# Later fetches of branch operands and gates, reordered remainder products and a shorter way for the softmax sums in a one-layer mixer trunk

## The chip, the core and the metric

The kernel runs on one core of a Trainium2 chip. The metric is the device time of one execution in microseconds, the median of several runs. The engines of the core are named as in the profile: PE (TensorE, with PEld for its weight loads), DVE (VectorE), ACT (ScalarE), POOL (GpSimd) and SP (SyncE, which here issues nearly all DMA transfers).

## The reference, cut to what matters

One layer on 1024 tokens of width 1024, with 16 learned tokens put in front (1040 positions). One projection makes the inputs of four mixers, their gate paths and four merge gates; the mixers' outputs are projected back, gated, summed and projected once more.

```python
h = rms_norm(h_res, pre_norm_g[i])
z = h @ w_in[i]
(pv, pg, cq, ckv, kr, mg, cu, cg, sbcx, sg, gl) = split_cols(z)

y_a = (pool_mixer(pv, pool_w[i], pool_scale[i]) * silu(pg)) @ w_out_pool[i]
y_b = (mla_attention(cq, ckv, kr, ...) * silu(mg)) @ w_out_mla[i]
y_c = (conformer_conv(cu, ...) * silu(cg)) @ w_out_conf[i]
y_d = (short_conv(sbcx, sc_dw_w[i]) * silu(sg)) @ w_out_sc[i]

gts = sigmoid(gl + gate_bias[i]).reshape(b_, l_, N_BRANCH, D_MODEL)
m = gts[:, :, 0] * y_a + gts[:, :, 1] * y_b + gts[:, :, 2] * y_c + gts[:, :, 3] * y_d
h_res = h_res + rms_norm(m @ w_o[i], post_norm_g[i])
```

Inside `mla_attention`, eight heads attend causally over keys and values that come out of a normalised low-rank `ckv`:

```python
kv = (rms_norm(c_kv, kv_norm_g) @ w_ukv).reshape(b_, l_, MLA_HEADS, QK_NOPE + V_DIM)
s = jnp.einsum('bqhd,bkhd->bhqk', qb, k)
s = jnp.where(k_pos[None, :] <= q_pos[:, None], s, -jnp.inf)
p = jax.nn.softmax(s, axis=-1)
o = jnp.einsum('bhqk,bkhd->bqhd', p, v)
```

## The kernel before

Every product is made of float32 values split into a high part and a remainder, and a product of two such values is three matmuls: high by high, high by remainder, remainder by high. The kernel has three stages, each with its own pools. The first makes the input projection by products of 512 columns into the PSUM banks `ps_pa` to `ps_pd`, and in between them, in four `lane`s of small steps, the norms, convolutions and the keys, values and queries, which it writes to DRAM. The second is the attention over 8 heads by 2 halves of the queries (16 units, `seq`). In between its products stand those of three of the four branches (`fills`, 48 steps spread over 112 blocks): for each branch 8 output tiles `d` of two halves, six matmuls of 512 columns each into `ps_y`, with the weights `whl`, the branch's operand `bo` (two tiles of 1 MB) and the gate `th`. The third stage makes the attention's output projection (`ps_u`) and the last projection.

No instruction is placed by hand. Each call records an operation in a `Plan`, and `flush` then orders them all by a list scheduler of its own: each engine takes, of the operations that its own costs say are ready, the one that was recorded first (moved by `ahead`). `late(ns)` tells it that a result is there so much later, `slow(ns)` that a DMA's is, and `behind` ties a transfer to the PE operation recorded last before it. The chip then executes each engine's instructions strictly in that order. Of the transfers, no more than eight may be under way in the scheduler's account, and eight semaphores in turn hold them to that on the chip.

What the change touches:

- `rs_row`, lines 943 to 969: the inverse root of a row of mean squares. PE multiplies with `ones` into a narrow bank, DVE scales (`rs`), POOL raises to the power -0.5, and PE transposes the result back into a row. `task_kv` (line 1274) calls it three times for `ckv`.
- `attend(h, c)`, lines 1506 to 1544: one unit. For each block `j` of 128 keys, three score matmuls into `ps_s`, the exponential on ACT, a split into the tile `pt` (four buffers), and three matmuls into `ps_o`: two with the whole 128 columns of `v_` as weights, and one, the remainder's product, with 64. Row 64 of the output holds the softmax sum. Blocks on the causal diagonal have fewer query columns: the last five blocks of a unit have 512, 400, 272, 144 and 16. The last, of 16 keys, is one matmul with `pz` and `vs`. `copy(ol[h][:, c], po)` then evacuates the bank.
- `sums(h)`, lines 1546 to 1556: for heads 0 to 6, row 64 of `ol` goes to DRAM (`l_dram`), from there to `lc` on 32 partitions, DVE takes the reciprocal, `lc` goes to DRAM (`r_dram`) and comes back broadcast over 64 partitions as `rb`. `head_out` multiplies `ol` with `rb` into `op` on DVE, and for odd heads with the gate `smg` on POOL. The last head makes its sums on PE (`sums_pe`) instead.
- `fills`, line 1605: the operand of the next branch is fetched at the tile `d == 4` of the current one.
- the loop over the units, line 1669: the gate `smg` of an odd head is fetched at its first unit.

Of the kernel before, what the change touches and what calls it, by code (L numbers as in the profile page):

```python
# [25 lines left out]
ALU = mybir.AluOpType  # L26
# [4 lines left out]
P = 128  # L31
# [440 lines left out]
def trunk_kernel(ctx, tc, a):  # L472
# [467 lines left out]

    done = {"ckv", "kr"}

    def rs_row(sqs, of, scale=None, tag="x"):

        n = sqs[0].shape[1]
        p = min(n, P)
        if len(sqs) > 1:  # L950
            add(POOL, sqs[0], sqs[0], sqs[1])
        sq = sqs[0]
        pc = bank(tag)[:p, :n // p]
        for j in range(n // p):
            PE.matmul(pc[:, j:j + 1].in_order(), sq[:, p * j:p * (j + 1)], ones, start=True, stop=True,
                      skip_group_check=True)
        yield
        rs = col([P, 4], "rs")[:p, :n // p]
        DVE.tensor_scalar(rs, pc, 1.0 / of, EPS, op0=ALU.mult, op1=ALU.add)
        POOL.tensor_tensor(rs, rs, mhalf[:p, :n // p], op=ALU.pow)  # L960
        if scale:
            DVE.tensor_scalar(rs, rs, scale, None, op0=ALU.mult)
        yield
        out = bank(tag)[:, :n]
        for j in range(n // p):
            PE.transpose(out[:, p * j:p * (j + 1)], rs[:, j:j + 1].to_broadcast([p, P]), ident[:p, :p])
        yield
        return out
# [275 lines left out]
    def task_kv():  # L1244
# [27 lines left out]
        ACT.activation(sq, ckv, AF.Square)  # L1272
        yield
        for n0, n in CH_KV:
            rs = yield from rs_row([sq[:, n0:n0 + n]], P)
            DVE.scalar_tensor_tensor(ckv[:, n0:n0 + n], ckv[:, n0:n0 + n], par[:, R_KVG:R_KVG + 1], rs,
                                     op0=ALU.mult, op1=ALU.mult)
        yield
# [227 lines left out]
    def attend(h, c):  # L1506

        q_, k_, v_ = qt[h, c], kt[h % 2], vt[h % 2]
        po = bank("o")
        nj = 4 * c + 5  # L1510
        for j in range(nj):
            lo_ = max(512 * c, P * j - NM)
            n = 512 * (c + 1) - lo_
            kn = P if j < nj - 1 else NM
            ks = slice(P * j, P * j + kn)
            qs = slice(512 - n, 512)
            s = bank("s")[:kn, :n]
            PE.matmul(s, k_[:NA, 0, ks], q_[:NA, 0, qs], start=True, stop=False)
            PE.matmul(s, k_[:QK, 0, ks], q_[:QK, 1, qs], start=False, stop=False)
            PE.matmul(s, k_[:QK, 1, ks], q_[:QK, 0, qs], start=False, stop=True)  # L1520
            d0 = P * j - NM
            dl, dh = max(d0, 512 * c, 0), min(d0 + P, 512 * (c + 1))
            if dh > dl:
                sd = s[:, dl - lo_:dh - lo_]
                add(DVE, sd, sd, maskT[:kn, dl - d0:dh - d0])
            p32 = at.tile([P, 512], F32, tag="p32", bufs=3, name="p32")[:kn, :n]
            ACT.activation(p32, s, AF.Exp)
            o = po[:, lo_ - 512 * c:]
            if kn == NM:
                x = pz[(2 * h + c) % 3]  # L1530
                copy(x[:NM], p32)
                copy(x[64:], p32)
                sub(POOL, x[32:32 + NM], p32, f(x[:NM]))
                PE.matmul(o, vs[h % 2][:, c], x, start=False, stop=True, skip_group_check=True)
            else:
                pt_ = at.tile([P, 2, 512], F32R, tag="pt", bufs=4, name="pt")[:, :, :n]
                split(pt_[:, 0], pt_[:, 1], p32)
                PE.matmul(o, v_[:, j, :P], pt_[:, 0], start=(j == 0), stop=False, skip_group_check=True)
                PE.matmul(o, v_[:, j, :P], pt_[:, 1], start=False, stop=False, skip_group_check=True)
                PE.matmul(o[:64], v_[:, j, P:], pt_[:, 0], start=False, stop=False, skip_group_check=True)  # L1540
            yield
        if c == 0:
            ol[h] = at.tile([P, 2, 512], F32, tag="ol", bufs=2, name="ol")
        copy(ol[h][:, c], po)

    def sums(h):

        lc = at.tile([32, 32], F32, tag="lc", bufs=2, name="lc")
        rb = at.tile([64, 2, 512], F32, tag="rb", name="rb")
        with plan.slow(5000):  # L1550
            ld(l_dram[h].rearrange("(o n) -> o n", o=1), ol[h][64:65].rearrange("p j n -> p (j n)"))
            ld(lc, l_dram[h].rearrange("(p n) -> p n", n=32))
            DVE.reciprocal(lc, lc)
            ld(r_dram[h].rearrange("(p n) -> p n", n=32), lc)
            ld(rb.rearrange("p j n -> p (j n)"), r_dram[h].partition_broadcast(64))
        return rb[:, 0], rb[:, 1]
# [35 lines left out]
    def fills():  # L1592
# [9 lines left out]
        for bi, (gi, wname, b0) in enumerate(branches):  # L1602
            bo = [bos[bi, k] for k in range(2)]
            for d in range(KD):
                if d == 4 and bi < 2:
                    with plan.behind():
                        load_bo(bi + 1)
                th = fp.tile([P, NT], F32, tag="th", bufs=3, name="th")
# [51 lines left out]
    for i, (h, c) in enumerate(seq):  # L1660
        with plan.behind() if i else nullcontext():
            if i + 2 < len(seq):
                load_q(*seq[i + 2])
            if c == 0 and h + 1 < H:
                load_kv(h + 1)
                if i == 0:
                    with plan.behind():
                        load_v(1)
            if c == 0 and h % 2:
                smg[h] = at.tile([P, NT], F32, tag="smg", name="smg")  # L1670
                ld(smg[h], z_dram[f"mg{h // 2}"])
        for j, _ in enumerate(attend(h, c)):
# [260 lines left out]
```

## Time and profile before

| what | value |
|---|---|
| runs | 971.98, 972.14, 972.54 us; median 972.14 us |
| the profiled execution's own time | 970.57 us |
| its span, first to last instruction | 968.7 us |
| granted TensorE clock, mean | 0.997 |
| matmuls on PE | 5003 |
| DMA traffic | 203.06 MB, mean 210 GB/s |

In the profile a matmul's duration is modelled and overlaps that of the next one, so what a matmul costs is read from the distance of the starts: 12 matmuls of 512 columns in a row stand 2.72 us apart in the chain of waits. Nearly every operation is issued at one line of the kernel, line 362 in `issue`, so the rows are told apart by their tiles and not by their lines.

### The profile page before, as it was taken

Reading aid. Unit: us, or ns where it says so; the run is one execution under the profiler, and the core shown is the slowest. Engines: PE = TensorE matmul, PEld = TensorE weight load, DVE = VectorE, ACT = ScalarE, POOL = GpSimd, SP = SyncE. Lnnn points to the kernel's source line nnn. Section 1 sums busy time; section 2 is a strip of 40 time slices with the busy share of each in tenths; the row PEclk is TensorE's granted clock in tenths of the full one; section 3 lists DMA queues with packets and bytes.
Section 4 is the critical chain, followed back from the end, with each engine's and each line's share of the span. In section 5 each row is a group of like instructions: output and inputs, shape, how many; then the busy total and the mean of one; then the engine's idle time right before and its main releaser. Section 6 shows DMA issues by size and latency. Waiting matters only on the chain.

```text
span 968.7 us, 15229 instructions
## 1 busy us (share of the span) xinstructions
PE 953.4 (98%) x5003; PEld 810.9 (84%) x5003; DVE 703.8 (73%) x1113; ACT 450.8 (47%) x914; POOL 678.5 (70%) x628
## 2 busy tenths in 40 slices
PE   8999999999999999999999999999999999999996
PEld 8999899889888888888888888888888888788885
DVE  5956957978979985446554867346868887799867
ACT  7743244343344555444444444366375465225631
POOL 5957565666767797788779587565377686647965
PEclk9999999999999999999999999999999999999998
DMA  8145566677688677685656687799969863772644
GB/s 258 46 126 146 164 217 214 211 227 250 211 264 262 204 230 229 202 275 181 196 166 190 224 293 240 212 317 316 233 186 277 210 191 109 272 252 84 200 148 152
DMA packets 136343, 203.06 MB, mean 210 GB/s; under 512 B 19678, under 2 KB 83165, under 8 KB 135496
## 3 DMA queue, kind: packets, MB, share of 16 engines
q1 hardware_dynamic: 127288, 185.31, 62.5%
q10 hardware_dynamic: 8656, 15.74, 4.5%
q0 software_dynamic: 320, 1.05, 0.3%
q8 instruction: 39, 0.64, 0.3%
q14 instruction: 40, 0.33, 0.1%
HBM read 129.14 MB, written 72.90 MB: 209 GB/s over the span
## 4 chain that ended last, share of the span: by engine, by line
PE 85%; DVE 4%; DMA 4%; POOL 3%; issue 2%; ACT 1%; SPq 0%; DVEq 0%; POOLq 0%; ACTq 0%
PE ps_pa L362 15%; PE ps_pb L362 14%; PE ps_pc L362 14%; PE ps_o L362 9%; PE ps_u L362 8%; PE ps_y L362 7%; PE ps_s L362 7%; PE ps_pd L362 7%; PE ps_x L362 4%; DVE ps_w L362 1%; DMA qt<-q 1%; POOL S L362 1%; POOL A L362 1%; DMA whl<-w_out_pool 1%; DMA x<-in_x_dram 1%
## 5 line engine op out<-in xcount | busy, mean ns | idle before, releaser
L362 PE MATMUL ps_pb<-T,S 128*128 128x512 f32 (+2 forms) x792 | 173.6, 359 | 0.0
L362 PE MATMUL ps_pa<-B,A 128*128 128x512 f32 (+2 forms) x792 | 169.4, 359 | 0.0
L362 PEld LDWEIGHTS ps_pa<-B,A 128*128 128x128 f32 x792 | 134.3, 188 | 22.4 <-issue 1.0
L362 PEld LDWEIGHTS ps_pb<-T,S 128*128 128x128 f32 x792 | 134.5, 189 | 21.5 <-issue 0.5
L362 POOL TENSOR_TENSOR S<-ss,S 128x512 fp32r<-128x512 f32 x84 | 114.5, 1373 | 47.8 <-ACT S L362 46.9
L362 POOL TENSOR_TENSOR A<-raw,A 128x512 fp32r<-128x512 f32 x84 | 113.7, 1360 | 44.2 <-ACT A L362 43.0
L362 POOL TENSOR_TENSOR pt<-p,pt 128x512 fp32r<-128x512 f32 (+1 forms) x96 | 101.0, 1077 | 52.8 <-ACT pt L362 22.1
L362 DVE TENSOR_TENSOR u<-ps_pb,u 128x512 f32<-128x512 f32 (+2 forms) x66 | 40.3, 610 | 69.9 <-PE ps_pb L362 63.7
L362 DVE SCALAR_TENSOR_TENSOR ps_w<-conv,par,ps_w 128x512 f32<-128x512 f32 x116 | 87.2, 752 | 2.6
L362 PE MATMUL ps_y<-bo,whl 128*128 128x512 f32 x288 | 85.5, 405 | 0.8 <-DMA whl<-w_out_pool 0.8
L362 ACT ACTIVATE S<-ss 128x512 fp32r<-128x512 f32 x84 | 51.0, 629 | 74.4 <-DVE ss L362 49.7
L362 PE MATMUL ps_pc<-T,S 128*128 128x512 f32 (+1 forms) x396 | 85.2, 359 | 0.0
L362 PE MATMUL ps_pd<-T,A 128*128 128x512 f32 (+2 forms) x396 | 84.2, 358 | 0.0
L362 PE MATMUL ps_pc<-B,S 128*128 128x512 f32 (+1 forms) x396 | 84.0, 358 | 0.0
L362 ACT ACTIVATE p<-ps_s 128x512 f32<-128x512 f32 (+4 forms) x112 | 49.6, 444 | 59.9 <-PE ps_s L362 32.7
L362 PEld LDWEIGHTS ps_pd<-T,A 128*128 128x128 f32 x396 | 67.3, 189 | 10.8
L362 PEld LDWEIGHTS ps_pc<-T,S 128*128 128x128 f32 x396 | 66.7, 189 | 10.8
L362 PEld LDWEIGHTS ps_pc<-B,S 128*128 128x128 f32 x396 | 66.5, 189 | 10.4
L362 PE MATMUL ps_s<-qt,kt 100*128 100x512 f32 (+4 forms) x336 | 68.5, 325 | 1.0 <-DVE mxs L362 0.9
L362 PE MATMUL ps_o<-pt,vt 128*128 128x512 f32 (+7 forms) x288 | 67.6, 345 | 0.0
L362 PEld LDWEIGHTS ps_s<-qt,kt 100*128 100x128 f32 (+1 forms) x336 | 54.1, 176 | 12.0 <-DVE mxs L362 1.7
L362 ACT ACTIVATE A<-raw 128x512 fp32r<-128x512 f32 x84 | 51.9, 626 | 20.8 <-PE ps_pd L362 9.6
(281 smaller groups left out, 1905.0 us busy)
## 6 DMA issues: line engine op xcount, KB each, us to landing
raw<-in_w_in_dram SPq DMA_DIRECT2D x52, 512.0 KB
th<-th SPq DMA_DIRECT2D x32, 512.0 KB
th<-z ACTq DMA_DIRECT2D x60, 256.0 KB
v<-vhl SPq DMA_DIRECT2D x16, 384.0 KB
qt<-q SPq DMA_DIRECT2D x16, 384.0 KB
vt<-v SPq DMA_DIRECT2D x8, 768.0 KB
bo<-bo SPq DMA_DIRECT2D x6, 1024.0 KB
w_out_mla<-whl SPq DMA_DIRECT2D x16, 256.0 KB
```

The costliest lines, as they stand in the source:

```text
L362: getattr(self.handle[o["eng"]], o["op"])(*map(real, o["args"]), **{k: real(v) for k, v in o["kw"].items()})
```

## The change

Five edits. (1) `rs_row` takes a number `ns`, and `task_kv` passes 1500: the scheduler then takes both steps of the inverse root to be there 1500 ns later. (2) In `attend` the remainders' products of the last three 128-key blocks are kept in the list `thirds` and issued later: between the two products of the 144-column block, behind its second one, and behind the 16-column one. (3) The copy of the last head's output counts as 500 ns later. (4) `sums` goes from the SBUF row straight to the 32 partitions of `lc`; `l_dram` is no longer used. (5) The operand of the next branch is fetched at `d == 6`, and the gate of heads 1, 3 and 5 at the second unit of the head instead of the first.

```diff
-    def rs_row(sqs, of, scale=None, tag="x"):
+    def rs_row(sqs, of, scale=None, tag="x", ns=0):
...
-        DVE.tensor_scalar(rs, pc, 1.0 / of, EPS, op0=ALU.mult, op1=ALU.add)
-        POOL.tensor_tensor(rs, rs, mhalf[:p, :n // p], op=ALU.pow)
+        with plan.late(ns):
+            DVE.tensor_scalar(rs, pc, 1.0 / of, EPS, op0=ALU.mult, op1=ALU.add)
+            POOL.tensor_tensor(rs, rs, mhalf[:p, :n // p], op=ALU.pow)
...
-            rs = yield from rs_row([sq[:, n0:n0 + n]], P)
+            rs = yield from rs_row([sq[:, n0:n0 + n]], P, ns=1500)
...
         nj = 4 * c + 5
+        thirds = []
+
+        def rest(last=False):
+            PE.matmul(*thirds.pop(0), start=False, stop=last, skip_group_check=True)
+
...
-                PE.matmul(o, vs[h % 2][:, c], x, start=False, stop=True, skip_group_check=True)
+                PE.matmul(o, vs[h % 2][:, c], x, start=False, stop=False, skip_group_check=True)
+                rest(last=True)
...
                 PE.matmul(o, v_[:, j, :P], pt_[:, 0], start=(j == 0), stop=False, skip_group_check=True)
+                if j == nj - 2:
+                    rest()
                 PE.matmul(o, v_[:, j, :P], pt_[:, 1], start=False, stop=False, skip_group_check=True)
-                PE.matmul(o[:64], v_[:, j, P:], pt_[:, 0], start=False, stop=False, skip_group_check=True)
+                thirds.append((o[:64], v_[:, j, P:], pt_[:, 0]))
+                if j < nj - 4 or j == nj - 2:
+                    rest()
...
-        copy(ol[h][:, c], po)
+        with plan.late(500 if h == H - 1 else 0):
+            copy(ol[h][:, c], po)
...
-            ld(l_dram[h].rearrange("(o n) -> o n", o=1), ol[h][64:65].rearrange("p j n -> p (j n)"))
-            ld(lc, l_dram[h].rearrange("(p n) -> p n", n=32))
+            ld(lc, ol[h][64:65].rearrange("p j (a n) -> p (j a) n", n=32))
...
-                if d == 4 and bi < 2:
+                if d == 6 and bi < 2:
...
-            if c == 0 and h % 2:
+            if h % 2 and c == int(h < H - 1):
```

Since the scheduler orders everything anew, the order of the instructions differs on every engine from the first `rs` of `ckv` on. Three places show what matters.

The first is PE at the end of unit (head 0, second half). `ps_o` is the output bank, `pt` the split exponentials, `vt` the values, `pz` and `vs` the operands of the 16-column block; the first number after the names is the output's partitions, 64 for a remainder's product. Before:

```order
L362 MATMUL ps_o<-pt,vt_6875 128x272
L362 MATMUL ps_o<-pt,vt_6875 64x272
L362 MATMUL ps_o<-pt,vt_6875 128x144 x2
L362 MATMUL ps_o<-pt,vt_6875 64x144
L362 MATMUL ps_o<-pz_6929,vs_6861 128x16
L362 MATMUL ps_s<-qt,kt_6867 128x400 x3
```

and with the change:

```order
L362 MATMUL ps_o<-pt,vt_6875 128x272
L362 MATMUL ps_o<-pt,vt_6875 128x144
L362 MATMUL ps_o<-pt,vt_6875 64x400
L362 MATMUL ps_o<-pt,vt_6875 128x144
L362 MATMUL ps_o<-pt,vt_6875 64x272
L362 MATMUL ps_o<-pz_6929,vs_6859 128x16
L362 MATMUL ps_o<-pt,vt_6875 64x144
L362 MATMUL ps_s<-qt,kt_6867 128x400 x2
```

The two remainders' products of 400 and 272 columns now stand behind the two of 144, and the one of 144 behind that of 16.

The second is PE at the inverse roots of `ckv` in the first stage: `ones` by `sqk` makes the sums, `ident` by `rs` turns the roots back. Before:

```order
L362 MATMUL ps_x<-ones,sqk 128x1 x4
L362 MATMUL ps_pc<-B_325,S_1348 128x512 x9
L362 MATMUL ps_pa<-B_234,A_1412 128x256 x3
L362 MATMUL ps_x<-ident,rs 128x128 x4
L362 MATMUL ps_x<-ones,sqk 128x1 x4
L362 MATMUL ps_pa<-B_234,A_1412 128x256 x9
L362 MATMUL ps_pb<-T_564,S_1449 128x256 x8
L362 MATMUL ps_x<-ident,rs 128x128 x4
```

and with the change:

```order
L362 MATMUL ps_x<-ones,sqk 128x1 x4
L362 MATMUL ps_pc<-B_325,S_1348 128x512 x9
L362 MATMUL ps_pa<-B_234,A_1412 128x256 x12
L362 MATMUL ps_pb<-T_564,S_1449 128x256 x12
L362 MATMUL ps_pc<-T_531,S_1456 128x256
L362 MATMUL ps_x<-ident,rs 128x128 x4
L362 MATMUL ps_x<-ones,sqk 128x1 x4
L362 MATMUL ps_pc<-T_531,S_1456 128x256 x11
L362 MATMUL ps_pb<-T_316,S_1476 128x256 x12
L362 MATMUL ps_pd<-T_587,A_1505 128x256 x12
L362 MATMUL ps_pa<-B_257,A_1481 128x256 x8
L362 MATMUL ps_x<-ident,rs 128x128 x4
```

Nine 512-column and 25 256-column matmuls now stand between the first sums and their roots, where nine and three stood, and 43 between the second ones, where 17 stood.

The third is SP's queue early in the attention, where `whl<-w_out_pool` are the weights of the first branch, `bo` the operand of the second, `qt`, `kt`, `vt` and `vs` the tiles of the coming units, `smg` the gate of head 1. Before:

```order
L362 DMA smg<-z_mg_3488 128x1024
L362 DMA vt_6875<-v_2571 128x1536
L362 DMA vs_6861<-v_2571 16x2x128 x2
L362 DMA vs_6861<-v_2571 16x2x64
L362 DMA whl<-w_out_pool_987 128x512
L362 DMA th<-th_3863 128x1024
L362 DMA whl<-w_out_pool_1167 128x512
L362 DMA qt<-q_5195 96x1024
L362 DMA th<-th_4070 128x1024
L362 DMA whl<-w_out_pool_1408 128x512
L362 DMA l_7272<-ol 1x1024
L362 DMA bo<-bo_4590 128x2048
```

and with the change, first from the same `vt` on:

```order
L362 DMA vt_6875<-v_2611 128x1536
L362 DMA lc<-ol 32x1x32
L362 DMA whl<-w_out_pool_987 128x512
L362 DMA th<-th_3822 128x1024
L362 DMA whl<-w_out_pool_1167 128x512
L362 DMA th<-th_4100 128x1024
L362 DMA qt<-q_5020 96x1024
L362 DMA smg<-z_mg_3486 128x1024
L362 DMA whl<-w_out_pool_1408 128x512
```

and then, eight rows on, the place to which the operand of the second branch went:

```order
L362 DMA rb<-r_7339 64x1024
L362 DMA vs_6863<-v_2611 16x2x128 x2
L362 DMA vs_6863<-v_2611 16x2x64
L362 DMA vt_6904<-v_2611 128x1536
L362 DMA bo<-bo_4605 128x2048
L362 DMA bo<-bo_4808 128x2048
L362 DMA whl<-w_out_pool_1780 128x512
L362 DMA th<-th_4295 128x1024
L362 DMA lc<-ol 32x1x32
L362 DMA qt<-q_5020 96x1024
```

The gate moved from ahead of `vt` and the weights to behind them, and the pair `bo` from ahead of the tiles of head 3 to behind them.

## The prediction, made before the changed kernel was run

> **What bounds the kernel now.** I read the page first: the span, the busy time of each engine, and the chain.
>
> ```profile
> span 968.7 us, 15229 instructions
> PE 953.4 (98%) x5003; PEld 810.9 (84%) x5003; DVE 703.8 (73%) x1113; ACT 450.8 (47%) x914; POOL 678.5 (70%) x628
> ```
>
> PE is busy for all but 15.3 us, and nothing is dropped from its work by the change, so there are two ways to gain: take away what PE waits for, or put its matmuls in an order in which they stand closer. The waits of PE, and of its weight loads (PEld), come next, each row with total, times and longest:
>
> ```profile
> PE ps_s L362 <- DVE mxs L362: 0.9, 1, 0.9
> PE ps_y L362 <- DMA whl<-w_out_pool: 0.8, 1, 0.8
> PE ps_x L362 <- POOL rs L362: 0.3, 1, 0.3
> PE ps_s L362 <- DMA qt<-q: 0.3, 1, 0.3
> PEld ps_o L362 <- POOL pt L362: 0.5, 2, 0.3
> ```
>
> They are few and short, and each of the first four belongs to something that the change moves. Since modelled ends hide a part of a wait, I size them by the starts. The measure is a stretch of the chain without a wait (start, duration, what):
>
> ```profile
> 839.19 43.53 PE ps_u L362 x192
> ```
>
> 43.53 / 192 = 0.227 us for 512 columns, 0.443 ns a column. The windows (busy time of PE, PEld, DVE, ACT, POOL, then the granted clock, the share of the DMA engines and GB/s) show where transfers crowd:
>
> ```profile
> 650.00:690.00 40.00, 38.91 (x215) 32.54 (x214) 29.09 (x78) 22.22 (x56) 20.27 (x25) 1.00 1.00 286
> 690.00:740.00 50.00, 50.00 (x267) 41.98 (x266) 36.13 (x90) 27.50 (x65) 32.02 (x33) 1.00 0.78 226
> ```
>
> The clock is granted in full in both, so the clock is no term. From 650 to 690 us the DMA engines are full; behind that there is room.
>
> **The ends of the units.** Two ends of a unit in the timeline of PE, without and with branch products in between:
>
> ```profile
> 644.22 0.67 PE L362 MATMUL ps_o<-pt,vt 128*128 128x272 f32 x5
> 644.72 0.21 PE L362 MATMUL ps_o<-pz,vs 80*128 80x16 f32 x1
> 644.79 0.71 PE L362 MATMUL ps_s<-qt,kt 96*128 96x512 f32 x2
> 645.34 0.28 PE L362 MATMUL ps_s<-kt,qt 96*128 96x272 f32 x1
> ...
> 683.97 0.29 PE L362 MATMUL ps_o<-pt,vt 128*128 128x144 f32 x2
> 684.10 0.22 PE L362 MATMUL ps_o<-pz,vs 80*128 80x16 f32 x1
> 684.17 1.86 PE L362 MATMUL ps_y<-bo,whl 128*128 128x512 f32 x7
> 685.87 0.27 PE L362 MATMUL ps_s<-ident,mr 128*4 128x128 f32 x1
> ```
>
> The first group of five is 272 twice and 144 three times (the row joins them). From 644.22 to 645.34 are 1.12 us for 544 + 432 + 16 + 1024 = 2016 columns, which take 0.89 us: 0.23 us lost. From 683.97 to 685.87 are 1.90 us for 288 + 16 + 3584 = 3888 columns, 1.72 us: 0.18 us lost. I read it so: weights of 128 columns load in about 0.11 us, and only during the matmul just ahead. Behind a matmul of 144 columns (0.064 us) some 0.05 us stay uncovered, behind one of 16 nearly all (seven products from 684.17 take 1.70 us instead of 1.59). Weights of 64 columns need no more than 0.064 us: the two steps from 683.97, whose second matmul is the remainder's product with half the weights, take 0.13 us, twice 144 columns. In the new order the second 144 stands behind 400 columns, the 16 behind 272, and what is left is the last remainder behind the 16 (half weights, 0 to 0.06 us) and the next matmul behind that (0.05 us). So 0.10 of 0.20 us go, in 16 units: **-1.6 us**, all on PE's path. Its bounds: everything lost now is saved, 16 x 0.2 = 3.2 us; or nothing, if the order of short matmuls isn't what costs. On the side of a loss: three `pt` tiles of four are now held to the unit's end, so the next unit's split can wait. The `pt` row above has two such waits, 0.5 us together; I keep 0.5 us of loss as the lower bound.
>
> [...]
>
> **The inverse roots of `ckv`.** PE and POOL in the first stage:
>
> ```profile
> 110.51 0.52 PE L362 MATMUL ps_pa<-B,A 128*128 128x256 f32 x3
> 111.13 0.65 PE L362 MATMUL ps_x<-ident,rs 128*128 128x128 f32 x4
> 113.58 1.12 PE L362 MATMUL ps_pb<-T,S 128*128 128x256 f32 x8
> 115.00 0.65 PE L362 MATMUL ps_x<-ident,rs 128*128 128x128 f32 x4 [0.30 <-POOL rs L362]
> ...
> 110.05 1.02 POOL L362 TENSOR_TENSOR rs<-rs,mhalf 128x4 f32<-128x4 f32 x1
> 113.93 1.02 POOL L362 TENSOR_TENSOR rs<-rs,mhalf 128x4 f32<-128x4 f32 x1 [0.92 <-DVE rs L362]
> ```
>
> Three matmuls of 256 columns need 0.34 us and stand 0.62 apart from the transposes, eight need 0.91 and stand 1.42 apart: 0.28 + 0.51 us, of which a tenth is what matmuls run over their columns anyway. Both roots end (111.07, 114.95) just as the transposes start: POOL is what PE waits for. With 22 and 26 more matmuls of 256 columns in between (2.5 and 2.9 us) it is covered: **-0.7 us**; bounds -0.8 and 0, the latter if as much appears where the later `ckv` is needed. Nobody needs it soon: the attention, which reads the keys and values made of it, stands at 644 us in the rows above.
>
> **Gate, operand and the DMA waits.** PE's two waits for transfers, with the transfers in the chain (start, duration from issue to landing) and SP's issues:
>
> ```profile
> 661.48 1.10 PE L362 MATMUL ps_y<-bo,whl 128*128 128x512 f32 x4
> 663.39 0.50 PE L362 MATMUL ps_y<-bo,whl 128*128 128x512 f32 x1 [0.81 <-DMA whl<-w_out_pool]
> 682.80 0.23 PE L362 MATMUL ps_o<-pt,vt 128*128 128x144 f32 x1
> 683.31 0.30 PE L362 MATMUL ps_s<-kt,qt 96*128 96x144 f32 x1 [0.28 <-DMA qt<-q]
> ...
> 656.37 6.98 DMA whl<-w_out_pool
> 671.64 11.54 DMA qt<-q
> ...
> 651.59 0.58 SPq L362 DMA_DIRECT2D smg<-z_mg  x1
> 663.87 0.80 SPq L362 DMA_DIRECT2D bo<-bo  x2
> ```
>
> Four products need 0.91 us and the fifth starts 1.91 behind the first: 1.0 us lost. At 682.80 a matmul of 0.064 us is followed after 0.51: 0.45 us. Ahead of that `whl` stood the gate of 512 KB, 1.8 us at 286 GB/s; ahead of that `qt` the operand pair of 2.1 MB, 7.3 us. In the new order neither is there, so `whl` would land about 661.6, ahead of its need at 662.4, and `qt` about 676: **-1.4 us**. Bounds: all of it gone, or both waits come back. On the losing side, the pair now stands ahead of two weight tiles, a gate and the `qt` four places on, and each pair can make a wait like the 0.45 us again, for two pairs 0.9 us. The second pair (`bi = 1`) waits for the first operand's buffers anyway and hardly moves.
>
> **The sums.** Of these seven chains I read first and last start, and at one place what the multiplications that end them do:
>
> ```profile
> L362 SPq DMA_DIRECT2D l<-ol x7: 230/231/246, 663.6 to 806.2; - x7
> L362 DVE TENSOR_TENSOR op<-ol,rb x14: 674/681/1775, 699.3 to 841.7; 64x512 f32<-64x512 f32 x14
> ...
> 773.91 0.86 PE L362 MATMUL ps_s<-qt,kt 100*128 100x512 f32 x3
> 775.70 0.45 PE L362 MATMUL ps_s<-qt,kt 100*128 100x400 f32 x1 [0.93 <-DVE mxs L362]
> ...
> 771.87 3.15 DVE L362 TENSOR_TENSOR op<-ol,rb 64x512 f32<-64x512 f32 x2
> 775.05 0.60 ACT L362 ACTIVATE ol<-ps_o 128x512 f32<-128x512 f32 x1 [1.84 <-DVE op L362]
> ```
>
> A chain takes 36 us (663.6 to 699.3), so a transfer less is not on PE's path by itself. What is: a pair of multiplications took 3.15 us where two of the median take 1.36, because of 1775 ns for one; the maxima `mxs` queue behind it on DVE and `ol` on ACT waits for it, since the buffers of `ol` are two. PE lost 1.79 - 3 x 0.227 = 1.1 us there. With one transfer less the scheduler can put the pairs earlier, ahead of the next use of that buffer. I take **-0.8 us**. Bounds: 1.1 us saved, or 1.1 us lost, a pair hitting such a place once more. The new transfer moves 32 runs of 128 bytes, as the second of the two old ones did, so I give it no price of its own; in SP's queue one issue per head falls away.
>
> **The last head.** Its copy counting 0.5 us longer puts more products ahead of the transposes:
>
> ```profile
> 819.69 2.65 PE L362 MATMUL ps_y<-bo,whl 128*128 128x512 f32 x11
> 822.38 0.46 PE L362 MATMUL ps_s<-ident,ol 64*128 64x64 f32 x4
> ```
>
> Eleven products need 2.49 us, and 2.69 pass: **-0.2 us**, bounds 0 and 0.4 (both halves).
>
> **New waits.** The scheduler orders anew everything from 109 us on. It made the order of before with the same costs, and that has the five waits above, 0.3 to 0.9 us each. I expect three of the middle size, 0.4 us: **+1.2 us**, by bounds 0 and 4 us (all five again with their totals, 2.8 us, and three of 0.4 us).
>
> **The sum** is -1.6 - 0.7 - 1.4 - 0.8 - 0.2 + 1.2 = -3.5 us. The profiled execution took 970.57 us, so 967.1; it lies 1.57 us under the median of 972.14, so by the median **968.6 us**.
>
> **Rivals.** (a) *The short matmuls aren't helped*: either the loads don't hide as I read them, or held `pt` tiles give it back. For it: I worked from two ends, with a few hundredths of us in each; against it, both lose the same. Then 968.6 + 1.6 = 970.2 us. [...] (b) *The waits only move*: the named ones go, and as many come elsewhere, since DMA stays at 0.78 behind 690 us and POOL and DVE at 70 and 73%. Then only the unit ends stay, 972.14 - 1.6 + 0.9 (the two pairs) = 971.4 us. (c) *The pair and the gates collide with the queries, and it is slower*. A transfer behind a pair took 11.54 us from issue to landing and was late by 0.45. With a gate of 1.8 us in front too, as heads 3 and 5 may have it, it is late by 2.3. If that strikes at both pairs, 4.6 us come on top, the DMA and DVE terms (2.2 us) fail, and 972.14 - 3.5 + 2.2 + 4.6 = 975.4 us. It decides from where a `qt` has less than 11.5 us between the release of its buffer and its first use. Against it: the order shows the pair behind `vt` and four places ahead of the next `qt`, not just ahead of a late one. (d) *The change does nothing at a place it names*: so for the second pair, as said; the gate of head 7 stays.
>
> **How the numbers follow.** The forecast has 0.55 (its own range 966.0 to 970.2), (a) 0.13, (b) 0.17, (c) 0.15. The range goes from 965.6 (unit ends at 2.5 us, half of the new waits, DVE's wait wholly gone, and some) to 972.8, which takes in (a) and (b) and leaves out most of (c). A difference of 0.2%, 1.9 us, is about what can be told from none, so faster ends at 970.2: faster is 0.54 of the forecast, 0.07 of (a) and 0.04 of (b), 0.65 together; within 0.2% 0.20; slower 0.15, (c).
>
> **What would show it.** Right: at the ends of the units, from the 272 columns to the first long matmul behind the 16, starts that stand 0.1 us closer; no `POOL rs` among PE's waits; no `whl<-w_out_pool` and no `qt` row among its DMA waits between 650 and 690 us; no ACT `ol` behind DVE `op`. Wrong: an unchanged loss at the unit ends (a); new rows of `qt`, `whl` or `vt` among PE's waits behind 690 us, with issue-to-landing times of 10 us and over (c); PE waits in the first stage behind 120 us, where before had next to none, would say that the new order as such is what costs.

## The result

The changed kernel takes 969.62 us (median of 20 runs, 968.81 to 971.11) beside 971.97 us (20 runs, 970.25 to 976.07) of the kernel before on the same chip. The ratio is 0.9976 with a 95% interval of 0.9969 to 0.9983: faster by 2.35 us, where 3.5 were forecast. The profiled execution took 968.91 us.

The page of the changed kernel, span and busy times:

```profile
span 967.1 us, 15247 instructions
...
PE 950.4 (98%) x5003; PEld 808.9 (84%) x5003; DVE 696.0 (72%) x1113; ACT 449.1 (46%) x914; POOL 678.0 (70%) x628
```

and what PE waits for (total, times, longest), of which the first row lies in the start-up, which the change doesn't touch:

```profile
PE ps_x L362 <- DVE x L362: 2.2, 1, 2.2
...
PE ps_s L362 <- ACT p L362: 1.0, 1, 1.0
PE ps_y L362 <- DVE th L362: 0.9, 1, 0.9
PE ps_y L362 <- POOL rs L362: 0.5, 2, 0.3
...
PE ps_x L362 <- DVE rs L362: 0.3, 1, 0.3
PE ps_o L362 <- ACT ol L362: 0.2, 1, 0.2
```

None of the four named waits of before is left: no `mxs`, no `whl`, no `qt`, and the `POOL rs` row now stands at another bank, `ps_y` instead of `ps_x`. Five new rows have come. To size both I cut the execution at four starts on PE, which every kernel here has: the first sums for `ckv` (`ones` by the squares of kv), the first score into `ps_s`, the first product into `ps_u`, the last matmul. The distances of these starts, in us:

| kernel | start-up | first stage from `ckv` on | attention | output stage | tail | span |
|---|---|---|---|---|---|---|
| before | 107.52 | 530.30 | 201.21 | 120.13 | 9.56 | 968.7 |
| changed | 107.67 | 530.44 | 199.81 | 119.76 | 9.37 | 967.1 |

So the gain lies in the attention, 1.40 us, with 0.4 us in the output stage; the first stage gained nothing. These are two single executions, 1.66 us apart, of which that of before lay 1.40 us below its median and that of the changed kernel 0.71 us below: the other 0.7 us of the 2.35 are in no row here. In the attention I also summed, over PE's steps from start to start, what each takes beyond 0.443 ns a column. Steps that lose over 0.2 us, the waits, sum to 2.73 us before and 2.68 us now. The steps around the sixteen 16-column matmuls (eight ahead of each, its own and three behind; without the steps just counted as waits) lose 4.14 us before and 2.95 us now. Hence the attention's gain is for the most part that of the unit ends, 1.2 us, and as many waits came as went.

The unit end that the prediction read from 644.22 us, now:

```profile
644.93 0.36 PE L362 MATMUL ps_o<-pt,vt 128*128 128x144 f32 x2
645.12 0.18 PE L362 MATMUL ps_o<-pz,vs 80*128 80x16 f32 x1
645.16 0.26 PE L362 MATMUL ps_o<-pt,vt 128*64 128x144 f32 x1
645.25 0.44 PE L362 MATMUL ps_s<-qt,kt 96*128 96x512 f32 x1
645.53 0.29 PE L362 MATMUL ps_s<-kt,qt 96*128 96x272 f32 x1
```

From 644.93 to 645.53 are 0.60 us for 144 + 272 + 16 + 144 + 512 = 1088 columns, which take 0.48: 0.12 us lost. Over the same twelve steps as in the sum above, this end loses 0.16 us, where it lost 0.25. Of the loss that stays, 0.05 us is where the prediction put it, behind the last remainder: 0.28 us between the starts at 645.25 and 645.53, for 512 columns of 0.227 us.

The roots of `ckv` on PE, and two later roots in the same stage:

```profile
110.66 1.59 PE L362 MATMUL ps_pa<-B,A 128*128 128x256 f32 x12
112.08 1.60 PE L362 MATMUL ps_pb<-T,S 128*128 128x256 f32 x12
113.52 0.28 PE L362 MATMUL ps_pc<-T,S 128*128 128x256 f32 x1
113.64 0.60 PE L362 MATMUL ps_x<-ident,rs 128*128 128x128 f32 x4
...
315.63 1.07 PE L362 MATMUL ps_pa<-B,A 128*128 128x512 f32 x4
316.99 0.62 PE L362 MATMUL ps_x<-ident,rs 128*128 128x128 f32 x4 [0.30 <-DVE rs L362]
...
574.51 2.45 PE L362 MATMUL ps_pa<-B,A 128*128 128x512 f32 x10
577.29 0.65 PE L362 MATMUL ps_y<-ident,rs 128*128 128x128 f32 x4 [0.33 <-POOL rs L362]
```

Twenty-five matmuls of 256 columns stand 2.98 us apart from the transposes and need 2.84: the wait of `ckv` is gone. But at 316.99 four products of 0.91 us are followed after 1.36, and at 577.29 ten of 2.27 us after 2.78. With a third such place at 382.7 us the losses are 0.46 + 0.31 + 0.49 = 1.26 us. The kernel before lost 0.12 + 0.29 + 0.00 us ahead of the same three groups of transposes, the 0.29 here, where two products of 0.45 us are followed after 0.74:

```profile
372.09 0.62 PE L362 MATMUL ps_pc<-T,S 128*128 128x512 f32 x2
372.83 0.65 PE L362 MATMUL ps_y<-ident,rs 128*128 128x128 f32 x4
```

So the new order, which put these transposes closer behind their sums, lost 0.85 us more at them, about what it gained at the roots of `ckv` (0.83 us lost ahead of their transposes before, 0.10 now).

In the attention the new waits are at the pairs of head 3 (PE, then ACT, POOL and DVE) and of head 6; a head's pair of multiplications comes when the scores of a later one run:

```profile
768.56 0.23 PE L362 MATMUL ps_s<-qt,kt 100*16 100x16 f32 x3
769.74 0.42 PE L362 MATMUL ps_s<-kt,qt 96*128 96x328 f32 x1 [0.95 <-ACT p L362]
770.38 1.88 PE L362 MATMUL ps_o<-pt,vt 128*128 128x512 f32 x7 [0.22 <-ACT ol L362]
...
769.18 0.50 ACT L362 ACTIVATE p<-ps_s 128x400 f32<-128x400 f32 x1 [1.09 <-POOL pt L362]
769.73 0.60 ACT L362 ACTIVATE ol<-ps_o 128x512 f32<-128x512 f32 x1
...
764.91 1.29 POOL L362 TENSOR_TENSOR m<-m,th 128x512 f32<-128x512 f32 x1
766.16 4.66 POOL L362 TENSOR_TENSOR pt<-p,pt 128x512 fp32r<-128x512 f32 x3
...
767.02 2.68 DVE L362 TENSOR_TENSOR op<-ol,rb 64x512 f32<-64x512 f32 x2
...
834.47 1.29 DVE L362 TENSOR_TENSOR op<-ol,rb 64x512 f32<-64x512 f32 x2
835.68 0.67 DVE L362 SCALAR_TENSOR_TENSOR th<-th,ps_y 128x512 f32<-128x512 f32 x1
...
836.41 0.98 PE L362 MATMUL ps_y<-bo,whl 128*128 128x512 f32 x3 [0.91 <-DVE th L362]
```

At the pair of head 3 PE loses 1.10 + 0.50 us by its starts, and an `op` pair stands beside POOL's remainders again, and takes 2.68 us instead of 1.36, while three remainders take 4.66 instead of 3 x 1.29 = 3.87. Why they take longer side by side these rows don't show. The pair of head 6 stands ahead of a `th` that PE needs for its bank: 1.08 us.

### The profile page after: what moved, and what is told of

It reads as the page before. It is cut to its first block, busy times and chain, and to the rows that moved or that the text cites. A ratio compares the mean times of both kernels' runs of the same rounds, so it can differ in the third digit from the quotient of the medians.

```text
span 967.1 us, 15247 instructions
## 1 busy us (share of the span) xinstructions
PE 950.4 (98%) x5003; PEld 808.9 (84%) x5003; DVE 696.0 (72%) x1113; ACT 449.1 (46%) x914; POOL 678.0 (70%) x628
## 3 DMA queue, kind: packets, MB, share of 16 engines
q0 software_dynamic: 320, 1.05, 0.3%
## 4 chain that ended last, share of the span: by engine, by line
PE 90%; POOL 3%; DVE 2%; issue 2%; ACT 1%; DMA 1%; DVEq 0%; SPq 0%; POOLq 0%; ACTq 0%
PE ps_pa L362 16%; PE ps_pb L362 16%; PE ps_pc L362 15%; PE ps_o L362 9%; PE ps_y L362 8%; PE ps_s L362 8%; PE ps_pd L362 7%; PE ps_u L362 7%; PE ps_x L362 5%; POOL S L362 1%; POOL lsq L362 1%; ACT junk L362 1%; DVE c L362 0%; DMA lacc<-acc 0%; POOL u L362 0%
## 5 line engine op out<-in xcount | busy, mean ns | idle before, releaser
L362 PE MATMUL ps_pa<-B,A 128*128 128x512 f32 (+2 forms) x792 | 171.7, 360 | 0.0
```

Of the source, the lines that this page charges most:

```text
L362: getattr(self.handle[o["eng"]], o["op"])(*map(real, o["args"]), **{k: real(v) for k, v in o["kw"].items()})
```

## The experiments

Two theories stood against each other. *Mine*: four parts have a gain of their own (unit ends, transfers, `ckv` roots, `op` pairs), and the new order gave some back by chance. *The rival* is (b) of the prediction: only the unit ends gain, and waits at full engines are conserved in whatever order.

### One part at a time, with the order of before

In these four the recorded order of the kernel before is kept row for row, and only the rows named are permuted, with what hangs on them (at the `ckv` roots two multiplications on DVE), so nothing else is ordered anew. Each has one profile, whose attention also scatters by itself, so the losses at the named places carry more than the length of the stretch. The unit ends (PE, shown at one of the sixteen):

```diff
+ps_o<-pt,vt 128x272
+ps_s<-qt,kt 128x512 x2
+ps_o<-pt,vt 128x272
+ps_o<-pt,vt 128x144
 ps_o<-pt,vt 64x400
-ps_o<-pt,vt 128x272
-ps_s<-qt,kt 128x512 x2
-ps_o<-pt,vt 128x272
+ps_o<-pt,vt 128x144
 ps_o<-pt,vt 64x272
-ps_o<-pt,vt 128x144 x2
+ps_o<-pz,vs 128x16
 ps_o<-pt,vt 64x144
-ps_o<-pz,vs 128x16
```

> The order of the kernel before, kept row for row on every engine; only the three remainders' products at the end of each unit stand where the change puts them. Theory A (weights load only during the matmul just ahead, so a short one can't cover the next load): the loss from the last 272 columns to the first long matmul behind the 16 falls from 0.2 to 0.1 us in each of 16 units, -1.6 us, about 970.5 against 972.1. Rival (weight loads are pulled ahead over several matmuls, or held pt tiles give it back): 0 us.

Measured: ratio 0.9992 (0.9978 to 1.0007), attention 200.01 us. By time alone this can't be told from no change. The steps around the 16-column matmuls lose 3.17 us instead of 4.14: a gain of 1.0 us that stands on 16 places.

The transfers (SP; the gate eight issues later, the operand pair behind the next unit's values):

```diff
-DMA smg<-z_mg 128x1024
 DMA vt<-v 128x1536
...
 DMA qt<-q 96x1024
+DMA smg<-z_mg 128x1024
...
-DMA bo<-bo 128x2048
-DMA bo<-bo 128x2048
...
 DMA vs<-v 16x2x64
+DMA bo<-bo 128x2048
+DMA bo<-bo 128x2048
```

> The order of the kernel before on every engine; only on SP the gate of head 1 goes eight transfers back, behind qt, and the first operand pair eleven back, behind vt and vs of head 3. Theory A (each of PE's two DMA waits is worth what its starts showed): the whl wait of 1.0 us near 663 and the qt wait of 0.45 us near 683 go, -1.4 us, 970.7. Rival B (a wait that is taken away comes back at the next transfer): the two waits go and others of 1 to 1.5 us come, within 0.3 us of before.

Measured: ratio 0.9987 (0.9979 to 0.9996), attention 200.35 us, 0.86 shorter. PE's wait for `qt` is gone, that for `whl` went from 0.8 to 0.5 us only. That lies between the two expectations, 1.4 us and 0.3.

The `ckv` roots (PE, in the first stage):

```diff
 ps_pa<-B,A 128x256 x3
-ps_x<-ident,rs 128x128 x4
 ps_x<-ones,sqk 128x1 x4
-ps_pa<-B,A 128x256 x9
+ps_pa<-B,A 128x256 x5
+ps_x<-ident,rs 128x128 x4
+ps_pa<-B,A 128x256 x4
 ps_pb<-T,S 128x256 x8
-ps_x<-ident,rs 128x128 x4
...
+ps_pc<-T,S 128x256 x4
+ps_x<-ident,rs 128x128 x4
```

> The order of the kernel before; only the transposes of the three roots of ckv, and what hangs on them, stand 5, 8 and 4 matmuls of 256 columns later on PE. Theory A: PE doesn't wait for POOL there, -0.7 us. In the changed kernel 0.8 us were gained there and lost again before the attention, at roots that the new order put close behind their sums; since the order is kept here, PE should reach the attention 0.7 us earlier than before. Rival B: the time is lost again elsewhere in the first stage, 0 at the attention's start.

Measured: ratio 1.0002 (0.9991 to 1.0013); from `ckv` to the attention 530.37 us, no gain. `POOL rs` is gone from the waits, and this one is new in the first stage (PE, then DVE):

```profile
117.06 0.40 PE L362 MATMUL ps_pd<-T,A 128*128 128x256 f32 x2
118.11 0.38 PE L362 MATMUL ps_pb<-T,S 128*128 128x256 f32 x1 [0.66 <-DVE u L362]
...
116.98 0.74 DVE L362 SCALAR_TENSOR_TENSOR ckv<-ckv,par,ps_x 128x512 f32<-128x512 f32 x1
117.64 0.42 DVE L362 TENSOR_TENSOR u<-ps_pb,u 128x256 f32<-128x256 f32 x1
```

The multiplication by the root came later on DVE, and with it `u`, which frees a bank: 0.8 us, as much as was gained. At this place the rival is right. (The attention of this one profile took 204.05 us in the order of before. A `whl` came 1.93 us late instead of 0.98, and a granted clock of 0.58 behind it, from 666 to 670 us, cost another 1.6 us; see the last section.)

All three permutations together:

> The three moves of the runs before at once, with the order of before otherwise. Theory A: -1.6 - 1.4 - 0.7 = -3.7 us against before, 968.4, 1 to 1.5 us faster than the changed kernel, whose new order gave some back. Rival B: about -1.6 us, no faster than the changed kernel.

Measured: 969.03 us, ratio 0.9975 (0.9966 to 0.9983), attention 198.72 us, 2.49 shorter; the waits left in it are `mxs` alone. Neither expectation is met: the ratio is that of the changed kernel, where *mine* had it 1 to 1.5 us faster, but the two DMA waits, 1.43 us, did not come back, as the rival had it. So ends and transfers together give what the whole change gives, without its edit of the sums and without its new order.

### The later roots

The changed kernel with its own order, and three groups of transposes three matmuls later (two shown):

```diff
-ps_pa<-B,A 128x512 x4
+ps_pa<-B,A 128x512 x7
 ps_x<-ident,rs 128x128 x4
-ps_pa<-B,A 128x512 x8
+ps_pa<-B,A 128x512 x5
...
-ps_pa<-B,A 128x512 x10
+ps_pa<-B,A 128x512 x12
+ps_pc<-B,S 128x512
 ps_y<-ident,rs 128x128 x4
```

> The changed kernel with its order kept, but three groups of four transposes of inverse roots (in its profile at 317.0, 382.7 and 577.3 us) stand three matmuls of 512 columns (0.68 us) later on PE. Theory (the ckv term of 0.7 us is there, and the new order gave it back by putting these transposes too close behind their sums, with losses of 0.46, 0.31 and 0.49 us): the three losses go, the stretch from the first kv sums to the attention shrinks from 530.44 to about 529.2 us, and the time is 1.2 us below the changed kernel's 969.6, at 968.4. Rival (the wait moves on to other work of VectorE, as in the run with the roots alone): the stretch stays at 530.4 and the time at 969.6.

Measured: 968.41 us, ratio 0.9969 (0.9957 to 0.9981). None of the three losses is left; the first of them on PE:

```profile
315.35 1.75 PE L362 MATMUL ps_pa<-B,A 128*128 128x512 f32 x7
316.93 0.60 PE L362 MATMUL ps_x<-ident,rs 128*128 128x128 f32 x4
```

Seven products stand 1.58 us ahead of their transposes and need 1.59. The stretch is 529.62 us. In all six kernels that have this edit it lies between 529.52 and 529.66, and in the three with the change's own places between 530.38 and 530.47: 0.8 us, shown. That is 0.7 us below the kernel before, but not the `ckv` term alone: 0.4 us of what the kernel before lost at these later transposes is gone too, and some 0.5 us have come in other steps of the stage, spread too thin to name.

### The sums

The changed kernel with its edit of the sums undone, two transfers through DRAM; the order up to the attention stays, that of the attention is made anew:

```diff
-            ld(lc, ol[h][64:65].rearrange("p j (a n) -> p (j a) n", n=32))
+            ld(l_dram[h].rearrange("(o n) -> o n", o=1), ol[h][64:65].rearrange("p j n -> p (j n)"))
+            ld(lc, l_dram[h].rearrange("(p n) -> p n", n=32))
```

> The changed kernel without its edit of the sums: these go through DRAM in two transfers again, as before. The order up to the attention is the same; in the attention the scheduler orders anew. Theory (a transfer more or less in a chain of 36 us is worth nothing by itself, and the 0.8 us that I forecast for it hung on where a pair of op multiplications falls): the time is within 1 us of the changed kernel's 969.6, with a pair of op that runs beside POOL's remainders or not, as it happens, and one loss of about 1 us for each pair that does. Rival (the single transfer is what moved the pairs onto bad places, so the edit costs its 2.7 us): the attention shrinks by 2 us or more, to below 198, and the time is near 967.0. Rival of the other sign (the single transfer does save what I forecast): 970.4 or more.

Measured: 971.29 us, ratio 1.0000 (0.9988 to 1.0012), attention 201.80 us: the rival of the other sign. PE's losses by starts are 1.69 us (the pair of head 6 ahead of a `th`), 1.29 us (a `qt`), 1.57 us (a pair beside remainders, now that of head 2) and 0.38 us. The `qt`, with its issue on SP:

```profile
681.99 0.33 SPq L362 DMA_DIRECT2D qt<-q  x1
...
693.58 0.47 PE L362 MATMUL ps_y<-bo,whl 128*128 128x512 f32 x1
695.09 0.39 PE L362 MATMUL ps_s<-kt,qt 96*128 96x328 f32 x1 [1.04 <-DMA qt<-q]
```

It took 13.0 us to land, behind the operand pair: the collision of the prediction's rival (c), in a kernel that is the change but for one transfer. So the single transfer is worth 2.0 us of attention here; by time its interval and that of the changed kernel (0.9969 to 0.9983) lie apart. None of the four losses is a wait for the sums themselves: what moved is where pairs and queries fall. That this would be so in another order isn't shown, and the run with all three permutations had the gain of the whole change with two transfers.

### The pairs of `op`

First the pairs of heads 3 and 6 moved at once, in the changed kernel's order (DVE):

```diff
 mr<-mxs 128x4
+op<-ol,rb 64x512 x2
 lc<-lc 32x32
 ps_s<-ps_s,maskT 128x112
-ps_s<-ps_s,maskT 128x128 x2
-op<-ol,rb 64x512 x2
-ps_s<-ps_s,maskT 128x128
+ps_s<-ps_s,maskT 128x128 x3
...
 op<-ol,ps_s 64x512
-op<-ol,rb 64x512 x2
 th<-th,ps_y 128x512
 m<-m,th 128x512
 th<-th,ps_y 128x512
 m<-m,th 128x512
 th<-th,ps_y 128x512
+op<-ol,rb 64x512 x2
```

> The changed kernel with its order kept, but two pairs of op multiplications moved on VectorE: that of head 3 (767.02, 2.68 us for two) to behind the mr reduction that ends at 764.85, ahead of the masks, and that of head 6 (834.47) behind three th further on. Theory (the pair beside three remainders on POOL slows both, and ACT's p, then PE, wait for them; that of head 6 holds back the th that frees a bank of ps_y): PE's losses at 768.6 and 769.7 (1.10 + 0.50) and at 835.1 (1.08) go, the attention shrinks from 199.81 to about 197.2 us, and the time is 2.6 us below the changed kernel's, at 967.0. Rival (VectorE and POOL have no room for the pair at that place, so the loss only moves): the attention stays within 0.7 us of 199.8, and the time at 969.6.

Measured: 974.74 us, ratio 1.0035 (1.0022 to 1.0047), 5 us slower than the changed kernel. The attention is shorter (198.60), but the output stage takes 126.25 us instead of 119.76:

```profile
841.20 0.73 PE L362 MATMUL ps_u<-boM,whl 128*128 128x512 f32 x2 [1.92 <-ACT boM L362]
843.45 6.88 PE L362 MATMUL ps_u<-boM,whl 128*128 128x512 f32 x18 [1.51 <-POOL boM L362]
...
838.84 3.33 POOL L362 TENSOR_TENSOR op<-op,smg 128x512 f32<-128x512 f32 x2 [8.18 <-DVE op L362]
842.13 2.49 POOL L362 TENSOR_TENSOR boM<-op,boM 128x512 fp32r<-128x512 f32 x2
```

I had left out what comes behind the pair: POOL's gate product and the split into `boM`, 5.8 us, which PE needs for its first products of the output stage. And at the pair of head 3 PE still lost 0.53 + 1.05 + 0.34 us by starts. With the later roots added:

> The changed kernel with the three groups of transposes later and the two pairs moved. Theory (the two losses lie in different stages and add): 1.2 + 2.6 us below the changed kernel, 965.8, which would be below both kernels. Rival (both only move): 969.6. If one of the two is right, 967.0 or 968.4.

Measured: 975.25 us, ratio 1.0039 (1.0026 to 1.0052). The first stage has its 0.8 us (529.63), the output stage the same loss (126.18).

Next, at the pair of head 3, the other suspect alone: POOL's addition `m` behind the remainders (with the later roots, as are all that follow):

```diff
 pt<-p,pt 128x512
-m<-m,th 128x512
 pt<-p,pt 128x512 x3
+m<-m,th 128x512
 op<-op,smg 128x512 x2
```

On SP the fetch of the next `th`, which waits for this addition, goes behind one other transfer with it.

> The changed kernel with the transposes later (as in the run with the roots later, 968.4) and, at head 3, POOL's addition m (764.91, 1.29 us in the changed kernel's profile) behind the three remainders pt that it stood ahead of. Theory (what ACT's p, and behind it PE, wait for at 768.6 and 769.7 are those remainders on POOL, which the addition holds back by 1.3 us; where the op pair stands matters less, as its move to another place changed this wait little): the losses of 1.09 + 0.50 us shrink by 1.0 to 1.3 us, the attention from 200.0 to about 198.9, time 967.3. Rival (the pair of op on VectorE slows POOL's remainders at whatever place, and the wait for p comes from that): the losses stay over 1.2 us, time 968.4.

Measured: 968.98 us, ratio 0.9975 (0.9962 to 0.9988), attention 200.01 us. Neither theory fits: the wait for `p` is gone, and one for `ol`, behind the pair, is as long (ACT, then PE; 1.73 us by starts):

```profile
769.28 0.60 ACT L362 ACTIVATE ol<-ps_o 128x512 f32<-128x512 f32 x1 [1.72 <-DVE op L362]
...
769.93 3.27 PE L362 MATMUL ps_o<-pt,vt 128*128 128x512 f32 x13 [1.49 <-ACT ol L362]
```

So two releasers come up together there. Both moved at once, the pair as in the first of these runs and the addition as above:

> The changed kernel with the transposes later and both edits at head 3 at once: the op pair behind the mr reduction and ahead of the masks on VectorE, and POOL's addition m behind the three remainders. Theory (PE's loss of 1.59 us at 768 to 770 has two releasers that come up together: ACT's p behind POOL's remainders, and ACT's copy ol behind VectorE's pair; with the pair moved 1.27 us of waits for p were left, with the addition moved 1.73 us for ol): with both moved the loss is below 0.4 us, the attention 1.2 us or more shorter than 200.0, at 198.8 or less, and the time 1.2 us below the 968.4 of the run with the transposes later. Rival (VectorE and POOL are full there and any order loses as much): the loss stays above 1.2 us, the attention at 200.0, time 968.4.

Measured: 968.98 us, ratio 0.9973 (0.9961 to 0.9985), attention 199.96 us: the rival. At 768 to 770 us PE loses 0.36 + 0.34 us now, and 0.93 us five microseconds on:

```profile
775.04 0.93 PE L362 MATMUL ps_o<-pt,vt 128*128 128x512 f32 x3 [0.77 <-POOL pt L362]
```

1.63 us in sum, where the changed kernel has 1.59, the run with the addition moved 1.73 and that with the pair moved 1.92. What looks alike in the four is POOL. The windows from 764 to 778 us (busy time of PE, PEld, DVE, ACT, POOL) of the changed kernel, and then of this one:

```profile
764.00:778.00 14.00, 12.82 (x67) 10.30 (x66) 11.46 (x25) 10.30 (x22) 14.00 (x12) 1.00 0.58 169
```

```profile
764.00:778.00 14.00, 12.94 (x66) 10.18 (x65) 11.16 (x25) 9.96 (x22) 13.90 (x12) 1.00 0.55 154
```

POOL has next to no gap there: remainders, an addition, two gate products and `boM`. That a full POOL is the cause is not shown, though. The window starts just behind a long gap (changed kernel):

```profile
763.65 1.30 POOL L362 TENSOR_TENSOR pt<-p,pt 128x512 fp32r<-128x512 f32 x1 [5.10 <-ACT pt L362]
```

Three kernels also speak against it. With the three permutations POOL is busy for 14.00 of the same 14 us, and PE loses 1.05 us; the kernel before loses 1.09 with POOL busy for 11.98. And with two transfers for the sums the same loss of 1.57 us stands at head 2, with POOL busy for 11.98 of the 14 us from 740 on and idle for 1.38 us right behind its remainders. What the runs show is that each of four orders of these two places lost 1.6 to 1.9 us, at changing releasers. A run that takes work off POOL in this stretch wasn't made, so the cause stays open.

The last pair, split around the `th`, with POOL making the first half of `boM` ahead of its second `op`:

```diff
 th<-th,ps_y 128x512
-m<-m,th 128x512
 op<-ol,ps_s 64x512
-op<-ol,rb 64x512 x2
+op<-ol,rb 64x512
 th<-th,ps_y 128x512
+m<-m,th 128x512
 m<-m,th 128x512
 th<-th,ps_y 128x512
+op<-ol,rb 64x512
```

> The changed kernel with the transposes later and, at head 6, the first multiplication of the op pair one addition earlier on VectorE and the second two th later, with POOL making the first half of boM ahead of its second op. Theory (PE's loss of 1.08 us at 835.1 comes from a th that stands behind the pair, and moving the whole pair behind failed only because boM came too late): the loss shrinks to 0.4 us or less, no wait for boM comes up, and the time is 0.7 to 1.0 us below 968.4, at 967.6. Rival (VectorE is full there, so th or boM is late in any order): the sum of PE's losses between 834 and 845 stays at 1 us or more, time 968.4 or above.

Measured: 969.33 us, ratio 0.9978 (0.9965 to 0.9991). The loss at `th` has gone from 1.08 to 0.27 us by starts, and one of 1.12 us for `boM` has come: the rival again.

```profile
842.28 1.90 PE L362 MATMUL ps_u<-boM,whl 128*128 128x512 f32 x7 [0.84 <-POOL boM L362]
```

Addition and split together:

> The changed kernel with all three: transposes later, POOL's addition behind the remainders, the last pair split. Theory (three separate losses that add): 969.6 - 1.2 - 1.1 - 0.8 = 966.5 us, with PE's waits behind the start-up below 1 us in sum, so below both kernels. Rival (only the transposes help): 968.4.

Measured: 969.76 us, ratio 0.9975 (0.9962 to 0.9987), no better than either. The kernel with the later roots alone has the lowest median of all, 968.41 us. Its interval overlaps that of the changed kernel, and the four later runs that keep its edit have ratios of 0.9973 to 0.9978 beside 0.9976, so by time it isn't shown to be the faster one. What is shown is a first stage 0.8 us shorter.

## Why the prediction was right, and where its sum was not

Faster by more than 0.2% was the likeliest case; it came out at 0.24%, with an interval that reaches down to 0.17%, and the time lies 1.0 us above the forecast, inside the range. What was expected held for the unit ends and the DMA waits, 2.6 us together. That the whole came as near is partly luck: the term of the sums and pairs came with the other sign, 2.4 us off, and 0.4 us in the output stage and 0.7 us of scatter between profiles and medians, which no term had, made up for part of it. Term by term:

- **Unit ends, -1.6 us.** That the order of the short matmuls costs is shown: with nothing else changed (the first run) the ends lose 1.0 us less, in the change 1.2 us less. The size was too high: 0.06 to 0.075 us an end, not 0.10. I read two ends, left 0.10 of 0.20 us at each and carried that over to sixteen; over twelve steps around each they lost 0.26 us and now lose 0.18. The reading behind it, that weights load only during the matmul just ahead, fits the profile of before, where the load for the branch product behind the 16 columns starts at 684.14 us, just behind the start of those at 684.10; no run tests it apart from the order. Rival (a) falls.
- **`ckv` roots, -0.7 us.** The wait went, and at these roots the size is right (0.83 us lost ahead of their transposes, now 0.10). That the stage in the run with the later roots is shorter by the same 0.7 us (530.30 to 529.62) is in part chance, since 0.4 us of it lies at other roots. In the change itself the stage came to +0.1. The step that failed is its lower bound, "if as much appears where the later `ckv` is needed": I looked for the loss behind `ckv`, and it came at three other roots, and in the run with the roots alone at `u` on DVE. The sign of being wrong that it names, PE waits in the first stage behind 120 us, did show.
- **Gate, operand and DMA waits, -1.4 us.** Both waits are gone from the changed kernel, 0.98 + 0.45 us by starts. In the run with the transfers alone 0.86 us came; `whl` was still 0.67 us late. Rival (c) didn't strike in the change, but did where the sums went the old way.
- **The sums and the pairs, -0.8 us.** This step failed in its mechanism. It took the loss of 1.1 us to be that of a badly placed pair, which an earlier one would cure. The change has 1.59 us at the same head and 1.08 at another, +1.6 us instead of -0.8, and three other placements at head 3 and two at head 6 didn't lower it. The bound below was there (1.1 us lost), and was passed. The edit itself still has a gain, since the change without it is 2.0 us longer in the attention; but there a `qt`, a `th` and another pair cost PE more, not a chain of sums.
- **Last head, -0.2 us.** Not singled out by any run. In the profiles the step just ahead of its first transposes loses 0.09 us instead of 0.20, that ahead of the second 0.10 as before, and the eleven steps ahead lose no less than they did (0.24 beside 0.20): at most 0.1 us.
- **New waits, +1.2 us.** Mis-sized: beside the pairs' there are the 1.26 us at the three roots, 0.85 us more than before lost there. Three waits of the middle size was about the right price for the first stage alone; the attention had its own.

Rival (b) describes the attention as a sum: its large waits sum to 2.73 us before and 2.68 after. What (b) lacks is that the transfers' part of them need not have come back: the run with three permutations kept it, with an attention of 198.72 us. Only the run with both pairs moved had a shorter one, 198.60, at the cost of its output stage. And 0.4 us in the output stage, from 120.13 us to between 119.72 and 119.78 in the changed kernel and the four runs of it in which the last pair wasn't moved, was in no term. Before, three steps from 936 us on lose 0.17 + 0.11 + 0.08 us, and now none loses over 0.04; what that comes from wasn't tried.

## What to carry to other kernels

Where a scheduler orders everything anew, price the new waits at the total of the old ones, and let a run with the old order kept row for row tell the edit from the shuffle. Before crediting the removal of a wait, look for what would be the next to release the same engine: in four orders here a wait changed its name and hardly its length (1.59 to 1.92 us). A busy time over a window of 14 us didn't tell which places those were. In this kernel short matmuls were better put between long ones, so that fewer weight loads have a short one ahead of them: 1.0 us less was lost at its sixteen unit ends with nothing else changed.

## What the runs showed of the hardware that I had not expected

In two runs the granted clock fell behind gaps of PE of about 2 us, to 0.51 and to 0.58. In the run with both pairs moved, PE stood still for 2.1 and 1.7 us between 839 and 843.5 us, by its starts. The windows (the value ahead of the DMA share is the granted clock):

```profile
836.00:843.00 7.00, 4.01 (x17) 2.66 (x15) 4.99 (x7) 1.26 (x2) 4.16 (x3) 0.93 1.04 402
843.00:849.00 6.00, 5.55 (x13) 4.36 (x14) 2.07 (x3) 2.19 (x4) 3.26 (x5) 0.51 0.38 126
849.00:855.00 6.00, 6.00 (x28) 4.93 (x27) 4.37 (x7) 1.15 (x2) 0.96 (x1) 1.00 0.69 227
```

From 843 to 849 us the granted clock was 0.51 (0.89 over the 32 us from 838, and 0.89 again in the run with the later roots added): thirteen products started in the 6 us from 843 instead of 28, by starts 0.427 us each instead of 0.227, a further 2.7 us. That is why waits of 3.8 us made the output stage 6.5 us longer. The gap of 1.1 us at the same place in the run with the split pair left the clock at 1.00.

In the run with the `ckv` roots it fell behind one gap, of 1.93 us by starts at the late `whl`, with no other over 0.6 us in the 20 us ahead of it (PE's row behind the gap, then the window):

```profile
665.97 4.27 PE L362 MATMUL ps_s<-qt,kt 100*128 100x512 f32 x11
666.00:670.00 4.00, 4.00 (x12) 3.17 (x11) 0.05 (x1) 2.90 (x5) 1.61 (x2) 0.58 1.04 242
```

The eleven matmuls, to the next start at 670.08, take 4.11 us instead of 2.50: 1.6 us, more than the late tile itself had added. Yet the wait of 2.2 us for the first `x` in the changed kernel's start-up left the clock at 1.00. So the length of a gap alone doesn't tell here whether the clock falls; what does, these runs don't show.

And single profiles scatter more than the effects looked for. Over kernels whose start-up has the same order PE's wait for the first `x` took between 0.5 and 2.2 us (it lies in the column start-up of the table above), and in the run with the `ckv` roots alone, whose attention has the order of before, one `whl` came 1.93 us late instead of 0.98, and the clock behind it was 0.58. Differences of a stretch of PE's starts, seen in several kernels, carried the readings here further than the times.
